# A list scheduler inside the kernel: other costs, a lock between two engines, one engine at a time on a PSUM bank, another margin

## The chip, the cores and the metric

The kernel runs on one core of a Trainium2 chip. The core has five engines that each work through an instruction queue of their own, in order: TensorE (matmuls; PE in the profile, with its weight loads as PEld), VectorE (DVE), ScalarE (ACT), GpSimd (POOL) and SyncE (SP), which here only issues DMAs. An instruction that needs the result of another engine waits for a semaphore, and everything behind it in the same queue waits with it. TensorE writes its results into PSUM, an accumulator memory of eight banks per partition; a bank holds 128 x 512 float32 here. The metric is the time of one execution on the device in microseconds (us), lower is better.

## The reference

One layer of a decoder block on x of 512 tokens by 1024 features, float32. What is computed, cut to the parts that matter here:

```python
xn = rms_norm(x, norm_g)
z = xn @ w_in                                # one wide input projection, split among all below
y_a = fox_attention(rms_norm(qa), rms_norm(ka), va, fa + b_forget)   # 8 heads of 64, causal
y_b = rg_lru(xb, ...)                        # convolution, gates, linear recurrence
y_c = nsa_attention(rms_norm(qc), ...)       # 8 heads: compressed + selected + window attention
y_d = spatial_gating(ud, vd, ...)
ys = [y_a * silu(ga), y_b * silu(gb), y_c * silu(gc), y_d * silu(gd)]
merged = sum(sigmoid(mg[n]) * (ys[n] @ w_branch[n]) for n in range(4))
out = x + merged @ w_out
```

With 512 tokens, the selected attention of y_c takes all blocks and its window covers all keys, so each head of y_c is two ordinary causal attentions (named s and w in the kernel) and one over 31 compressed keys.

## The kernel before, in words

Every float32 operand of a matmul is split into a high part (a copy in the format fp32r) and a low part (operand minus high part), and a product is three matmuls: high by high, low by high, high by low. The split is the steady work of the other engines: ACT or POOL makes the high part, DVE the low part by a subtraction. A weight piece is 128 x 1024, fetched by one DMA of 512 KB into one of four buffers (`raw`), split into one of three pairs (`w`).

**The two kinds of TensorE work.** Dense work is the projections: blocks of 128 x 512 matmuls into a PSUM bank of the pool `z` (three banks), from `zgen` and `chunks`. Attention work is made of units, one per head of y_a (eight, named a) and two per head of y_c (sixteen, s and w). A unit runs: `scores` (matmuls into a bank `s`; DVE adds the mask and takes the maximum; ACT takes the exponential; POOL scales by the reciprocal of the sum, tile `p`), then `finish`: `transposes` in five pieces of two 128 x 128 blocks, each piece into one half of a bank `tb`; for each piece ACT copies the half to `ph` and DVE subtracts to `pl`; then `values` multiplies `ph` and `pl` with v into a bank `o`. `finish` of one unit is interleaved with `scores` of the next, and `fill(gap)` puts a stated amount of dense work between the steps. In the attention of y_a there is one bank `tb` with two halves, in that of y_c there are two banks.

**Who sets the order.** From the first projection to the end of the attention of y_c, the instructions are not issued as the program makes them. `order.on` is true, and every engine call goes to `Order.add`, which records the operation, its cost and what it needs: the operations that wrote or read overlapping areas. At some points (`shut`, and once at the end) `Order.settle` calls `Order.plan` and then issues the operations in the planned order. `plan` is a list scheduler. It keeps for each engine the time from which it is free, takes the engine that can start first, and gives it, among the operations whose needs are met at that time, the one that stands first in the program. An operation is ready when all it needs has ended plus `WAKE` of its own engine (a dictionary of waiting times; 1.2 us for PE, some hundredths for the others, 0.2 for POOL). The costs come from `Order.cost`, linear in the elements of the largest operand. Two matmuls that accumulate into one area have only their order kept, with no wait between them. So the plan's times are never used on the chip, only the order within each queue; the semaphores make it safe. On lines: every planned instruction carries the line of the issuing call in `settle`, L188, in the profile. Work outside the planned region (the warm-up, a few constants, and everything after the attention of y_c: recurrence, spatial gating, merges, output projection) is issued directly and has the line L201 of `_Engine.__getattr__`.

**What a wait covers.** The framework beneath the kernel puts a semaphore wait wherever two engines touch the same data, or the same bank of a PSUM tile, in the order in which the instructions are issued. The planner before knows areas, but neither the bank nor anything that two engines share.

Of the kernel before, what the change touches and what calls it, by code (L numbers as in the profile page):

```python
# [15 lines left out]
PSUM = bass.MemoryType.PSUM  # L16
# [50 lines left out]
class Order:  # L67


    WAKE = {"ACT": 0.036, "DVE": 0.033, "SP": 0.064, "POOL": 0.2, "PE": 1.2}  # L70

    def __init__(self, nc):
        self.eng = {"ACT": nc.scalar, "DVE": nc.vector, "POOL": nc.gpsimd, "PE": nc.tensor, "SP": nc.sync}
        self.on, self.ops, self.seen, self.ring, self.before, self.stacks = False, [], {}, {}, {}, {}
        self.free = dict.fromkeys(self.eng, 0.0)
        self.wire, self.end, self.pending, self.queued = 0.0, {}, [], None

    def pool(self, real, stack):
        p = _Pool(self, real)
        self.stacks.setdefault(id(stack), []).append(p)  # L80
        return p

# [13 lines left out]
    def add(self, name, method, args, kw):  # L96
        aps = [(n == 0, a) for n, a in enumerate(args)] + [(k in ("out", "accum_out"), a) for k, a in kw.items()]
        aps = [(w, a) for w, a in aps if isinstance(a, bass.AP)]
        n, need = len(self.ops), {}
        boxes = [(w, *self.area(a)) for w, a in aps]  # L100
        for w, t, *box in boxes:
            if w and t in self.before:
                need.update((m, True) for m, *_ in self.seen.get(self.before[t], ()))
            for m, w2, b in self.seen.get(t, ()):
                if (w or w2) and box[0] < b[1] and b[0] < box[1] and box[2] < b[3] and b[2] < box[3]:
                    need[m] = need.get(m, False) or not (name == "PE" == self.ops[m][0] and w and w2)
        if self.queued is not None and self.ops[self.queued][0] == name:
# [3 lines left out]
        self.ops.append((name, method, args, kw, need, self.cost(name, kw, aps), {b[1] for b in boxes}))  # L111
        self.pending.append(n)
        return n

    @staticmethod
    def cost(name, kw, aps):

        free = max(a.free_size() for _, a in aps)
        scalar = any(not w and x.free_size() == 1 for w, x in aps)
        if name == "PE":  # L120
            return max(0.112, free / 2400 + 0.018), free / 2400 + 0.175
        if name == "SP":
            return 0.37, aps[0][1].partition_size() * free * 4 / 330e3
        if name == "DVE":
            t, over = 0.17 + free / 850 + 0.06 * scalar, 0.08
        elif name == "ACT":
            t, over = 0.15 + free / 1140 + 0.09 * scalar + 0.12 * ("accum_out" in kw), 0.09
        else:
            two = sum(not w and x.free_size() == free for w, x in aps) > 1
            t, over = (0.3 + free / 430 if two else 0.2 + free / 1100 + 0.1 * scalar), 0.02  # L130
        return t - over, t

    def plan(self):

        ops, left, then, ready = self.ops, {}, {}, {}
        soon, able = {e: [] for e in self.eng}, {e: [] for e in self.eng}
        free, wire, end, out = dict(self.free), self.wire, self.end, []
        for i in self.pending:
            name, need = ops[i][0], ops[i][4]
            ready[i], left[i] = 0.0, 0  # L140
            for m, whole in need.items():
                if m in end:
                    ready[i] = max(ready[i], end[m] + self.WAKE[name] if whole else 0.0)
# [5 lines left out]
        done = {}  # L149
        for _ in self.pending:  # L150
            best = None
            for e in self.eng:
                t = free[e]
                while soon[e] and soon[e][0][0] <= t:
                    heapq.heappush(able[e], heapq.heappop(soon[e])[1])
                c = (t, e) if able[e] else (soon[e][0][0], e) if soon[e] else None
                best = min(best, c) if best and c else best or c
            t, e = best
            while soon[e] and soon[e][0][0] <= t:
                heapq.heappush(able[e], heapq.heappop(soon[e])[1])  # L160
            i = heapq.heappop(able[e])
            busy, whole = ops[i][5]
            free[e] = t + busy
            if e == "SP":
                wire = max(wire, t + 1.6) + whole
                done[i] = wire + 0.6
            else:
                done[i] = t + whole
            out.append((i, t, free[e], wire, done[i]))
            for j in then.get(i, ()):  # L170
                f = ops[j][0]
                ready[j] = max(ready[j], done[i] + self.WAKE[f] if ops[j][4][i] else t)
                left[j] -= 1
                if not left[j]:
                    heapq.heappush(soon[f], (ready[j], j))
        return out

    def settle(self, stack=None):

        if not self.pending:  # L180
            return
        out = self.plan()
        if stack is not None:
            names = {t for p in self.stacks.get(id(stack), ()) for t in p.names}
            out = out[:max((k + 1 for k, o in enumerate(out) if self.ops[o[0]][6] & names), default=0)]
        for i, t, free, wire, done in out:
            name, method, args, kw, *_ = self.ops[i]
            getattr(self.eng[name], method)(*args, **kw)  # L188
            self.free[name], self.wire, self.end[i] = free, wire, done
        gone = {o[0] for o in out}  # L190
        self.pending = [i for i in self.pending if i not in gone]

# [10 lines left out]


class _Pool:
    def __init__(self, order, real):
        self.order, self.real, self.names, self.lines = order, real, [], {}

    def tile(self, *args, tag=None, bufs=None, **kw):
        if tag is not None:  # L210
            kw.update(tag=tag, bufs=bufs)
        t = self.real.tile(*args, **kw)
        self.names.append(t.tensor.name)
        if tag is not None:
# [8 lines left out]
def tile_hybrid_layer(ctx: ExitStack, tc: tile.TileContext, x, xT, units, small, bsp, out):  # L223
    nc = tc.nc
    order = Order(nc)
    ACT, DVE, POOL, PE, DMA = (_Engine(order, e) for e in ("ACT", "DVE", "POOL", "PE", "SP"))

    def pool(name, stack=ctx, **kw):
        return order.pool(stack.enter_context(tc.tile_pool(name=name, bufs=1, reuse_waits="tile", **kw)), stack)


    def behind(op):
# [709 lines left out]
    ug, ready = {}, []  # L942
# [799 lines left out]
```

## Time and profile before

| what | value |
|---|---|
| median of three runs | 725.02 us (724.39 to 725.21) |
| the profiled execution | 724.89 us |
| its span, first to last instruction | 723.2 us |
| TensorE busy | 703.2 us, 97% |
| VectorE busy | 575.8 us, 80% |
| ScalarE busy | 367.2 us, 51% |
| GpSimd busy | 167.7 us, 23% |
| planned region | about 5 to 395 us of the span |

How to read it: the span runs from the first instruction to the last; the execution's own time is 1.7 us longer. A busy share is the union of an engine's instructions as the profiler records them. Matmuls overlap in the records, so that a busy TensorE still can lose some tenths of a microsecond at a wait. A row of the wait view names the waiting engine and tile, the releaser, the total in us, how often, and the longest. A row of the view by windows gives, for one stretch, its length, each engine's busy time with its count of instructions, the granted TensorE clock as a share of full speed, the share of the DMA engines and their GB/s.

### The profile page before, as it was taken

How to read it: one execution, taken by the hardware profiler on the slowest of the kernel's cores; microseconds unless marked ns; L12 is line 12 of the kernel's file. 1: busy time of each engine (PE TensorE's matmuls, PEld its weight loads, DVE VectorE, ACT ScalarE, POOL GpSimd, SP SyncE). 2: the span in 40 equal slices, each digit the busy share in tenths (PEclk: the TensorE clock that was granted, in tenths of full speed). 3: DMA queues.
4: the chain of work that ended last, by engine and by line, in shares of the span. 5: the costliest groups of instructions: out<-in, count | busy, mean ns of one | idle time of the engine just before them, and what ended most of it. 6: DMA issues, size and time to landing. Idle time of an engine off the chain costs nothing.

```text
span 723.2 us, 9672 instructions
## 1 busy us (share of the span) xinstructions
PE 703.2 (97%) x3357; PEld 574.4 (79%) x3357; DVE 575.8 (80%) x1138; ACT 367.2 (51%) x725; POOL 167.7 (23%) x230
## 2 busy tenths in 40 slices
PE   8999999999998999989999999999999999999997
PEld 6888788777866888878887787888888888888876
DVE  6797866666489838888997979999868858958995
ACT  4452565664523336766665891434443551554641
POOL 4115552442445312323343322100000000000000
PEclk9999999999999999999999999999999999999999
DMA  8613222112112521200011223235432242143302
GB/s 321 239 43 116 76 89 70 59 59 76 42 59 88 175 90 57 88 30 30 30 59 43 76 87 102 88 109 182 145 118 88 85 138 98 36 139 117 116 30 87
DMA packets 20640, 68.35 MB, mean 95 GB/s; under 512 B 2416, under 2 KB 2800, under 8 KB 20592
## 3 DMA queue, kind: packets, MB, share of 16 engines
q1 hardware_dynamic: 20160, 67.25, 27.9%
q8 instruction: 26, 0.43, 0.2%
q10 hardware_dynamic: 432, 0.49, 0.2%
q14 instruction: 22, 0.18, 0.1%
HBM read 65.64 MB, written 2.10 MB: 94 GB/s over the span
## 4 chain that ended last, share of the span: by engine, by line
PE 75%; DVE 14%; ACT 8%; issue 2%; DMA 1%; POOL 0%; DVEq 0%; SPq 0%; ACTq 0%
PE pj L201 10%; PE tb L188 4%; PE z_ud L188 3%; PE z_qc L188 3%; PE z_ka L188 3%; PE z_gb L201 3%; PE z_qa L188 3%; PE z_va L188 3%; PE z_mg L201 3%; PE z_xb L188 3%; PE mg2y L201 2%; PE z_kv L188 2%; PE z_vd L188 2%; PE mg3y L201 2%; PE mg1y L201 2%; PE z_gd L188 2%
## 5 line engine op out<-in xcount | busy, mean ns | idle before, releaser
L201 PE MATMUL pj<-w_wb,yh 128*128 128x512 f32 x256 | 80.2, 390 | 0.0
L201 PEld LDWEIGHTS pj<-w_wb,yh 128*128 128x128 f32 x256 | 48.1, 188 | 10.4 <-ACT tm L201 0.4
L201 PE MATMUL pj<-w_wb,yl 128*128 128x512 f32 x128 | 49.8, 389 | 0.0
L188 DVE TENSOR_TENSOR pl_a<-tb,ph_a 128x256 fp32r<-128x256 f32 x40 | 16.1, 421 | 18.7 <-PE tb L188 8.0
L201 DVE TENSOR_TENSOR w_wb<-r_wb,w_wb 128x512 fp32r<-128x512 f32 x32 | 21.8, 713 | 9.5 <-ACT w_wb L201 8.5
L201 PEld LDWEIGHTS pj<-w_wb,yl 128*128 128x128 f32 x128 | 24.0, 188 | 4.9
L188 ACT CAST ph_a<-tb 128x256 fp32r<-128x256 f32 x40 | 14.2, 375 | 25.6 <-PE tb L188 21.9
L188 ACT ACTIVATE p_s<-p_s,nm_s 128x512 f32<-128x512 f32 (+3 forms) x32 | 17.9, 562 | 12.9 <-DVE nm_s L188 12.7
L188 PE MATMUL z_gd<-xh,w_gd 128*128 128x512 f32 x64 | 23.6, 415 | 0.5 <-DVE sgd L188 0.5
L188 POOL TENSOR_SCALAR p_w<-p_w,nm_w 128x128 f32<-128x128 f32 (+3 forms) x32 | 16.9, 546 | 27.1 <-DVE nm_w L188 27.1
L188 POOL TENSOR_SCALAR p_s<-p_s,nm_s 128x128 f32<-128x128 f32 (+3 forms) x32 | 17.2, 556 | 25.3 <-ACT ph_w L188 10.8
L188 DVE CUSTOM_DVE_ANT_0 p_a<-s_a,maskm 128x512 f32<-128x512 f32 (+3 forms) x32 | 15.5, 488 | 9.3 <-PE s_a L188 8.1
L188 PE MATMUL z_xb<-xh,w_xb 128*128 128x512 f32 x64 | 22.9, 415 | 0.0
L188 PE MATMUL z_ud<-xh,w_ud 128*128 128x512 f32 x64 | 22.7, 402 | 0.0
L188 ACT ACTIVATE p_a<-p_a,nm_a 128x512 f32<-128x512 f32 (+3 forms) x32 | 17.9, 561 | 9.4 <-DVE nm_a L188 9.1
L188 PE MATMUL z_ga<-xh,w_ga 128*128 128x512 f32 x64 | 22.0, 404 | 0.0
L188 POOL TENSOR_SCALAR p_a<-p_a,nm_a 128x128 f32<-128x128 f32 (+3 forms) x32 | 18.6, 598 | 14.8 <-DVE nm_a L188 14.8
L188 ACT ACTIVATE p_w<-p_w,nm_w 128x512 f32<-128x512 f32 (+3 forms) x32 | 18.0, 564 | 7.3 <-DVE nm_w L188 6.2
L201 PE MATMUL z_gb<-xh,w_gb 128*128 128x512 f32 x64 | 21.1, 391 | 0.0
L201 ACT CAST w_wb<-r_wb 128x1024 fp32r<-128x1024 f32 x12 | 12.6, 1048 | 15.5 <-issue 15.5
L188 DVE TENSOR_TENSOR pl_s<-tb,ph_s 128x256 fp32r<-128x256 f32 x40 | 16.0, 415 | 4.9 <-ACT ph_s L188 4.6
L188 ACT CAST ph_w<-tb 128x256 fp32r<-128x256 f32 x40 | 13.9, 369 | 11.3 <-PE tb L188 8.9
(812 smaller groups left out, 2336.1 us busy)
## 6 DMA issues: line engine op xcount, KB each, us to landing
r_wb<-in_units_dram SPq DMA_DIRECT2D x16, 512.0 KB, 3.8
xt<-in_x_dram SPq DMA_DIRECT2D x4, 512.0 KB, 8.8
r_ga<-in_units_dram SPq DMA_DIRECT2D x4, 512.0 KB, 3.6
r_gd<-in_units_dram SPq DMA_DIRECT2D x4, 512.0 KB, 3.8
r_ud<-in_units_dram SPq DMA_DIRECT2D x4, 512.0 KB, 4.4
r_gc<-in_units_dram SPq DMA_DIRECT2D x4, 512.0 KB, 3.7
r_xb<-in_units_dram SPq DMA_DIRECT2D x4, 512.0 KB, 3.6
r_gb<-in_units_dram SPq DMA_DIRECT2D x4, 512.0 KB, 3.6
```

Source lines behind the costliest of these rows:

```text
L188: getattr(self.eng[name], method)(*args, **kw)
L201: return lambda *args, **kw: real(*args, **kw).ins
```

## The change

All of it is in the planner; no operation is added to or removed from the kernel, and no engine is changed for any.

- `WAKE` of PE goes from 1.2 to 0.05 us, of POOL from 0.2 to 0.11. A new `MARGIN` adds 0.5 us for PE where the operation waited for is of another compute engine. So a PE operation that waits for DVE, ACT or POOL is ready 0.55 us after its planned end, where it was 1.2.
- `cost` gets other numbers. A PE operation is its columns over 2400 plus the load of its weights; DVE, ACT and POOL get other slopes and constants, POOL two forms. For DVE and POOL it also says whether the operation excludes the other engine: all of POOL but memsets; on DVE those with an operand of more than one element in SBUF and none in PSUM, but not reductions, reciprocals and memsets.
- `plan` keeps `shared`, the end and the engine of the last such operation. One that is placed on the other engine while it runs gets its end put off to after it.
- `plan` keeps `bank`, for each PSUM tile the engine that touched it last and when that ends. An operation of another engine on that tile is put back until then.
- `plan` models TensorE's weight loads by `load`, the time from which the array is free, and the DMA with 350 instead of 330 bytes per ns and other fixed times.

The core of the diff:

```diff
-    WAKE = {"ACT": 0.036, "DVE": 0.033, "SP": 0.064, "POOL": 0.2, "PE": 1.2}
+    WAKE = {"ACT": 0.036, "DVE": 0.033, "SP": 0.064, "POOL": 0.11, "PE": 0.05}
+    MARGIN = {"ACT": 0.0, "DVE": 0.0, "SP": 0.0, "POOL": 0.0, "PE": 0.5}
...
-    @staticmethod
-    def cost(name, kw, aps):
+    def cost(self, name, method, kw, aps):
 
         free = max(a.free_size() for _, a in aps)
         scalar = any(not w and x.free_size() == 1 for w, x in aps)
+        wide = [x for w, x in aps if not w and x.free_size() > 1]
         if name == "PE":
-            return max(0.112, free / 2400 + 0.018), free / 2400 + 0.175
+            weights = kw["lhsT"] if "lhsT" in kw else wide[0]
+            return aps[0][1].free_size() / 2400, 0.112 * max(64, min(128, weights.free_size())) / 128
         if name == "SP":
-            return 0.37, aps[0][1].partition_size() * free * 4 / 330e3
+            return 0.37, aps[0][1].partition_size() * aps[0][1].free_size() * 4 / 350e3
         if name == "DVE":
-            t, over = 0.17 + free / 850 + 0.06 * scalar, 0.08
-        elif name == "ACT":
-            t, over = 0.15 + free / 1140 + 0.09 * scalar + 0.12 * ("accum_out" in kw), 0.09
-        else:
-            two = sum(not w and x.free_size() == free for w, x in aps) > 1
-            t, over = (0.3 + free / 430 if two else 0.2 + free / 1100 + 0.1 * scalar), 0.02
-        return t - over, t
+            alone = bool(wide) and method not in ("tensor_reduce", "reciprocal", "memset") and not any(
+                x.tensor.name in self.psum for x in wide)
+            return 0.155 + free / 960 + 0.05 * scalar + 0.06 * (method == "tensor_tensor_scan" and free / 100), alone
+        if name == "ACT":
+            return 0.15 + free / 1140 + 0.09 * scalar + 0.15 * ("accum_out" in kw), False
+        if method == "memset":
+            return 0.1 + free / 1200, False
+        return (0.09 + free / 540 if len(wide) > 1 and method == "tensor_tensor" else 0.18 + free / 1170), True
+
+    OVER = {"ACT": 0.098, "DVE": 0.082, "POOL": 0.028}
...
+        margin = lambda e, m: self.WAKE[e] + (self.MARGIN[e] if ops[m][0] not in (e, "SP") else 0.0)
...
-            busy, whole = ops[i][5]
-            free[e] = t + busy
-            if e == "SP":
-                wire = max(wire, t + 1.6) + whole
-                done[i] = wire + 0.6
+            open_ = max((bank[x][1] + self.WAKE[e] for x in ops[i][7] if x in bank and bank[x][0] != e), default=0.0)
+            if open_ > t:
+                heapq.heappush(soon[e], (open_, i))
+                continue
+            a, b = ops[i][5]
+            if e == "PE":
+                start = max(t + b, load)
+                load, free[e], done[i] = start + a + 0.014, start + max(a - 0.098, 0.003), start + a + 0.172
+            elif e == "SP":
+                wire = max(wire, t + 1.3) + b
+                free[e], done[i] = t + a, wire + 0.86
             else:
-                done[i] = t + whole
-            out.append((i, t, free[e], wire, done[i]))
+                done[i] = t + a
+                if b:
+                    if shared[1] != e and shared[0] > t + 0.06:
+                        done[i] = shared[0] - 0.06 + a
+                    shared = done[i], e
+                free[e] = done[i] - self.OVER[e]
+            for x in ops[i][7]:
+                bank[x] = e, done[i]
...
-                ready[j] = max(ready[j], done[i] + self.WAKE[f] if ops[j][4][i] else t)
+                ready[j] = max(ready[j], done[i] + margin(f, i) if ops[j][4][i] else t)
```

More of the change, by code (lines that the diff above doesn't have):

```diff
@@ L75, in __init__, with pool @@
         self.free = dict.fromkeys(self.eng, 0.0)
-        self.wire, self.end, self.pending, self.queued = 0.0, {}, [], None
-    def pool(self, real, stack):
-        p = _Pool(self, real)
+        self.wire, self.shared, self.load, self.psum, self.bank = 0.0, (0.0, None), 0.0, set(), {}
+        self.end, self.pending, self.queued = {}, [], None
+    def pool(self, real, stack, psum):
+        p = _Pool(self, real, psum)
         self.stacks.setdefault(id(stack), []).append(p)
@@ L136, in plan @@
         soon, able = {e: [] for e in self.eng}, {e: [] for e in self.eng}
-        free, wire, end, out = dict(self.free), self.wire, self.end, []
+        free, end, out = dict(self.free), self.end, []
+        wire, shared, load, bank = self.wire, self.shared, self.load, dict(self.bank)
+        margin = lambda e, m: self.WAKE[e] + (self.MARGIN[e] if ops[m][0] not in (e, "SP") else 0.0)
         for i in self.pending:
@@ L142, in plan @@
                 if m in end:
-                    ready[i] = max(ready[i], end[m] + self.WAKE[name] if whole else 0.0)
+                    ready[i] = max(ready[i], end[m] + margin(name, m) if whole else 0.0)
                 else:
@@ L148, in plan @@
                 heapq.heappush(soon[name], (ready[i], i))
-        done = {}
-        for _ in self.pending:
+        done, todo = {}, len(self.pending)
+        while len(out) < todo:
             best = None
@@ L161, in plan @@
             i = heapq.heappop(able[e])
-            busy, whole = ops[i][5]
-            free[e] = t + busy
-            if e == "SP":
-                wire = max(wire, t + 1.6) + whole
-                done[i] = wire + 0.6
-            else:
-                done[i] = t + whole
-            out.append((i, t, free[e], wire, done[i]))
+            open_ = max((bank[x][1] + self.WAKE[e] for x in ops[i][7] if x in bank and bank[x][0] != e), default=0.0)
[9 more added lines that the diff above has]
+                free[e], done[i] = t + a, wire + 0.86
+            else:
+                done[i] = t + a
[6 more added lines that the diff above has]
+                bank[x] = e, done[i]
+            out.append((i, dict(free), wire, shared, load, done[i]))
             for j in then.get(i, ()):
                 f = ops[j][0]
-                ready[j] = max(ready[j], done[i] + self.WAKE[f] if ops[j][4][i] else t)
+                ready[j] = max(ready[j], done[i] + margin(f, i) if ops[j][4][i] else t)
                 left[j] -= 1
@@ L185, in settle @@
             out = out[:max((k + 1 for k, o in enumerate(out) if self.ops[o[0]][6] & names), default=0)]
-        for i, t, free, wire, done in out:
+        for i, self.free, self.wire, self.shared, self.load, self.end[i] in out:
             name, method, args, kw, *_ = self.ops[i]
+            self.bank.update((x, (name, self.end[i])) for x in self.ops[i][7])
             getattr(self.eng[name], method)(*args, **kw)
-            self.free[name], self.wire, self.end[i] = free, wire, done
         gone = {o[0] for o in out}
@@ L205, with __init__ @@
 class _Pool:
-    def __init__(self, order, real):
-        self.order, self.real, self.names, self.lines = order, real, [], {}
+    def __init__(self, order, real, psum):
+        self.order, self.real, self.psum, self.names, self.lines = order, real, psum, [], {}
     def tile(self, *args, tag=None, bufs=None, **kw):
@@ L213, in tile @@
         self.names.append(t.tensor.name)
+        if self.psum:
+            self.order.psum.add(t.tensor.name)
         if tag is not None:
@@ L228, in pool @@
     def pool(name, stack=ctx, **kw):
-        return order.pool(stack.enter_context(tc.tile_pool(name=name, bufs=1, reuse_waits="tile", **kw)), stack)
+        return order.pool(stack.enter_context(tc.tile_pool(name=name, bufs=1, reuse_waits="tile", **kw)), stack,
+                          kw.get("space") is PSUM)
     def behind(op):
```

3 lines of the change are left out of this document (2 added, 1 removed).

## The prediction

> **What bounds the kernel now.** I read the page first, then the busy times by windows cut at the kernel's stages, then TensorE's waits by stage, then the order of time around the longest of them. Head of the page, and its chain of waits by engine:
>
> ```profile
> span 723.2 us, 9672 instructions
> PE 703.2 (97%) x3357; PEld 574.4 (79%) x3357; DVE 575.8 (80%) x1138; ACT 367.2 (51%) x725; POOL 167.7 (23%) x230
> PE 75%; DVE 14%; ACT 8%; issue 2%; DMA 1%; POOL 0%; DVEq 0%; SPq 0%; ACTq 0%
> ```
>
> TensorE is busy for 97% of the span and makes up 75% of the chain. A new order cannot take work from it, so the change can win only what TensorE loses now. The windows (stretch, its length, busy PE, PEld, DVE, ACT, POOL, granted clock, DMA) say where that is:
>
> ```profile
> 6.40:85.00 78.60, 77.75 (x341) 62.51 (x342) 63.77 (x110) 36.43 (x61) 29.30 (x31) 1.00 0.42 152
> 85.00:205.00 120.00, 117.19 (x590) 94.95 (x589) 77.27 (x186) 69.09 (x165) 45.80 (x70) 1.00 0.22 71
> 205.00:245.00 40.00, 35.23 (x160) 27.74 (x160) 38.26 (x73) 13.16 (x24) 21.90 (x25) 0.96 0.35 110
> 245.00:270.00 25.00, 25.00 (x121) 20.64 (x121) 12.86 (x36) 7.04 (x18) 3.16 (x3) 1.00 0.36 119
> 270.00:395.00 125.00, 120.64 (x687) 100.06 (x687) 106.90 (x331) 81.44 (x238) 42.55 (x70) 1.00 0.15 47
> ```
>
> These five are the planned region, in order: first projections, attention of y_a, passage to y_c, dense, attention of y_c. TensorE idles 0.85, 2.81, 4.77, 0 and 4.36 us, together 12.8. What follows 395 us is not planned and keeps its order. VectorE has 38.26 of 40 us filled in the passage and 106.90 of 125 in the attention of y_c; in the attention of y_a 77.27 of 120.
>
> TensorE's waits in the region (waiting tile, releaser: total, times, longest), the first seven from the two attentions, the rest from before them and between:
>
> ```profile
> PE tb L188 <- DVE pl_a L188: 1.9, 4, 0.5
> PE tb L188 <- ACT ph_a L188: 0.5, 1, 0.5
> PE s_a L188 <- DVE q_a L188: 0.2, 1, 0.2
> PE tb L188 <- ACT ph_s L188: 1.1, 3, 0.4
> PE tb L188 <- DVE pl_s L188: 1.0, 1, 1.0
> PE tb L188 <- ACT pc L188: 0.8, 1, 0.8
> PE tb L188 <- ACT ph_w L188: 0.4, 2, 0.2
> PE s_s L188 <- DVE q_c L188: 2.9, 1, 2.9
> PE kt_s L188 <- POOL zkm L188: 1.1, 1, 1.1
> PE qt_c L188 <- POOL zq_c L188: 0.3, 1, 0.3
> PE z_kv L188 <- DVE v_a L188: 0.5, 1, 0.5
> PE z_kv L188 <- DVE w_kv.00_743 L188: 0.3, 1, 0.3
> ```
>
> Two families: transposes that wait until another engine has left the bank `tb`, 12 waits and 5.7 us; and work that DVE or POOL delivers late, 6 waits and 5.3 us. A wait costs a little more than its row, since a matmul's record reaches beyond its turn. Rows from the chain (start, length) and from the order of time:
>
> ```profile
> 132.50 2.77 PE z_qc L188 x12
> 133.89 0.76 DVE L188 TENSOR_TENSOR pl_a<-tb,ph_a 128x256 fp32r<-128x256 f32 x2
> 136.02 0.39 PE L188 MATMUL o_a<-pl_a,v_a 128*128 128x512 f32 x1
> ```
>
> Twelve matmuls take 2.77 us, 0.23 each, but one is shown with 0.39: 0.16 of every wait is hidden. (The other two rows are for the margin, below.)
>
> **The change part by part.** No instruction is added or removed, DMAs included, so every term is a wait that goes, comes or moves, and queues other than TensorE's matter only through what they hand to it.
>
> *One engine at a time on a bank.* This is what the first family looks like in order of time:
>
> ```profile
> 116.44 0.37 ACT L188 CAST ph_a<-tb 128x256 fp32r<-128x256 f32 x1 [1.72 <-PE tb L188]
> 116.86 0.33 PE L188 MATMUL tb<-identf,p_a 128*128 128x128 f32 x1
> 117.23 0.42 DVE L188 TENSOR_TENSOR pl_a<-tb,ph_a 128x256 fp32r<-128x256 f32 x1 [1.72 <-PE tb L188]
> 117.71 0.33 PE L188 MATMUL tb<-identf,p_a 128*128 128x128 f32 x1 [0.52 <-DVE pl_a L188]
> ```
>
> ACT reads one half, TensorE writes the first block of the other half, DVE reads the first half, TensorE writes the second block: four turns on one bank where the old plan sees two independent halves. The waits follow the issue order, so TensorE stands at 117.71 with dense matmuls queued behind it. The new plan puts the second block back until the bank is free and gives TensorE a dense matmul meanwhile; nothing is removed from the chain of the unit, since the bank's readers were ahead of it anyway. The family is worth 5.7 + 12 x 0.16 = 7.6 us, with short waits below the view's threshold (the attentions idle 2.81 + 4.36 = 7.2, their rows sum to 5.9 with s_a, some 1.3 more) 8.9. What covers the gain is dense work whose weights are already split; DVE, which splits them, has 43 us to spare in the first attention, but only 18 in the second. I take 70% of 7.6, **-5.3**, between 0 and -8.9.
>
> *The exclusion of DVE and POOL.* The order of time in the passage:
>
> ```profile
> 221.46 1.04 POOL L188 TENSOR_TENSOR zq_c<-zq_c,tsc 128x512 f32<-128x512 f32 x1
> 222.47 1.05 POOL L188 TENSOR_SCALAR w_gd<-r_gd 128x1024 fp32r<-128x1024 f32 x1
> 221.55 0.98 DVE L188 TENSOR_SCALAR sl<-sl 128x4 f32<-128x4 f32 x1
> 222.56 0.96 DVE L188 TENSOR_TENSOR sl<-sl 128x4 f32<-128x4 f32 x1
> 223.56 0.17 DVE L188 TENSOR_SCALAR sl<-sl 128x4 f32<-128x4 f32 x1
> 229.60 0.47 PE L188 MATMUL s_s<-ka_s,q_c 128*128 128x512 f32 x1 [2.86 <-DVE q_c L188]
> 230.60:234.00 3.40, 3.40 (x11) 2.82 (x10) 3.37 (x8) 1.41 (x4) 1.04 (x1) 0.50 0.34 104
> ```
>
> Four elements take DVE 0.98 and 0.96 us while POOL works, 0.17 right after. The old plan books the 0.17, so its DVE runs ahead of the real one, and it sends `s_s` to TensorE's queue 2.86 us too early, in front of dense z_gd. After that standstill the clock is granted at 0.50, the lower of its two levels, for 3.4 us: 1.7 us of work lost.
> The Trainium skill ("SBUF — State Buffer", section "Who interferes with whom") has the same lock: the one that starts first keeps the shared port for its whole instruction, the other stands still. These rows agree, 0.98 against 0.17; what the rule says beyond them comes with the rivals.
> The second family is worth 5.3 + 6 x 0.16 = 6.3 us. Knowing the lock does not shorten it: DVE is full there, and the plan can only fill TensorE's time with other blocks, of which each needs a DVE split too. I take 40%, **-2.5**, between 0 and -6.3; of the clock's 1.7 half, **-0.9**, between 0 and -1.7 (a stall of half the length may still be followed by a slow stretch).
>
> *The margin.* In the rows above, the low part ends at 133.89 + 0.76 = 134.65 and its matmul starts at 136.02, 1.37 later, with dense matmuls between: that is the old 1.2 at work. It goes to 0.55. As long as dense work fills the time, nothing is won by starting 0.65 earlier; at the first scores and first transposes of the two attentions, four places, 4 x 0.65 = -2.6 would be the most. What it may cost: each piece must now be on time within 0.55. The counts of transposes and evictions:
>
> ```profile
> L188 PE MATMUL tb<-identf,p_a x80: 270/272/332, 101.7 to 202.7; 128*128 128x128 f32 x80
> L188 DVE TENSOR_TENSOR pl_a<-tb,ph_a x40: 410/424/426, 104.1 to 203.4; 128x256 fp32r<-128x256 f32 x40
> ```
>
> 80 transposes are 40 pieces for the eight units of y_a; the sixteen units of y_c make 80 more: 120. Today 12 transposes are late, by 0.47 on average. Better costs should make errors smaller, the shorter margin lets more of them through. I take 12 new waits of 0.2 us, **+2.4**; at the upper end 21 of 0.66 (reckoned under the rivals), +13.9.
>
> *Costs of DMA and weight loads.* The first 78.6 us idle for only 0.85 and the diff's total for a 512 KB transfer hardly moves (1.6 + 1.59 + 0.6 against 1.3 + 1.50 + 0.86, all from the diff): **0**, at most +2 if the earlier stages, too, lose cover by the margin: three more waits of the size of z_kv's 0.5 + 0.16.
>
> Sum: -5.3 - 2.5 - 0.9 + 2.4 = -6.3. The profiled execution took 724.89 us (723.2 of span and 1.7 around it), 0.13 below the median of 725.02. So 718.6 on its scale, **718.7** on the median's.
>
> **The rivals.**
> *A, the whole pot.* All late work is foreseen and filled: -8.9 - 6.3 - 1.7 + 2.4 = -14.5, 710.5. For it: most waits stand directly in front of ready dense matmuls, as at 117.71. Against it: DVE's 38.26 of 40 in the passage.
> *B, VectorE sets the pace.* TensorE runs through its dense work sooner and meets unsplit weights later: only the waits of the first attention stay gone, their 1.9 + 0.5 and 5 x 0.16 (-3.2), and the +2.4 of the margin is paid: 724.2. For it: 106.90 of 125. Against it: 18 us of idle VectorE there, and dense z blocks lasting until the end of the region.
> *C, the lock's winner is guessed wrong* (the other side). The place is the handing over of `ph` and `pl` in both attentions. The old 1.2 us covers a whole POOL instruction (1.05); 0.55 does not. If DVE loses the port where the plan has it win, the piece is 1.05 - 0.55 = 0.5 late, and TensorE stands for 0.5 + 0.16. POOL is busy 45.80 of 120 and 42.55 of 125 us, about 36%, so 43 of the 120 pieces are exposed; if half of them lose, 21 x 0.66 = +13.9, and with the gains of -8.7 the time is 730.2. It decides from 8.7 / 0.66 = 13 such pieces on. For it: a matmul that waits takes the whole queue with it. Against it: the plan now knows of the lock at all, and `pl` itself reads PSUM.
> The page named above states what C rests on: who blocks is decided by which of the two is issued first, not by the kind of operation. The rows cannot show how often two queues come in the planned order.
>
> **How the numbers follow.** Forecast 0.47 (its own range 715 to 722), A 0.18, B 0.17, C 0.18. A measurement of this kernel can tell about 0.2%, 1.45 us, from no change. Faster: the forecast but for 0.02, all of A, a fifth of B: 0.66. Same: the rest of B and the forecast's 0.02, less 0.02 of B: 0.14. Slower: C and that 0.02: 0.20. The range goes from A's 710.5 to 729, short of C's end, and leaves out about 0.07 below and 0.10 above.
>
> **What would show it.** Right: of the `tb` rows about four waits and under 2 us are left; the wait of `s_s` for `q_c` is under 1.5 us; idle TensorE from 6.4 to the end of the region falls from 12.8 to 8; low parts are used some 0.6 after they end, not 1.4. B: the `tb` waits are gone, and in their place dense `z` matmuls wait for DVE. C: more `o` and `tb` waits than now, short, with DVE as releaser. Wrong in kind: `tb` still waits 12 times for half a microsecond, which would mean that the bank was not the cause; or the time is gained or lost after the planned region.

## The result, and the profile after

The changed kernel takes 716.2 us (median of 4 runs, 715.04 to 716.98) beside 724.9 us for the kernel before; the ratio is 0.9879, with a 95% interval of 0.9862 to 0.9897. By the ratio that is 8.8 us, 1.2%, faster. The forecast of 718.7 us was 2.5 us too high, and the sign and the range held. The experiments will show that the closeness of the sum is in part luck: one of its terms was wrong by 5 us, and the terms do not add.

The profiled execution took 716.89 us with a span of 715.2. The head of its page:

```profile
span 715.2 us, 9666 instructions
PE 700.1 (98%) x3357; PEld 573.8 (80%) x3357; DVE 571.3 (80%) x1138; ACT 365.3 (51%) x725; POOL 174.1 (24%) x230
```

The same 3357 matmuls are in it. The span is 8.0 us shorter: TensorE's idle time went from 723.2 - 703.2 = 20.0 to 715.2 - 700.1 = 15.1 us, and its "busy" time lost 3.1 us. No matmul became faster; the record of a matmul that is followed by a wait or has just waited is longer than its turn (the 0.16 us of the prediction), so fewer stalls also show as less busy time.

The windows (stretch, its length, then busy PE, PEld, DVE, ACT, POOL, granted clock, DMA share, GB/s):

```profile
6.40:85.00 78.60, 77.02 (x337) 61.65 (x338) 63.21 (x109) 36.31 (x61) 31.28 (x31) 1.00 0.41 151
85.00:205.00 120.00, 118.20 (x603) 97.66 (x601) 79.76 (x193) 69.69 (x167) 50.27 (x74) 1.00 0.22 71
205.00:245.00 40.00, 36.52 (x164) 28.60 (x165) 35.23 (x73) 12.72 (x26) 22.49 (x22) 0.96 0.41 132
245.00:270.00 25.00, 25.00 (x128) 20.76 (x127) 12.66 (x37) 6.85 (x19) 2.11 (x3) 1.00 0.33 105
270.00:387.00 117.00, 116.19 (x669) 96.94 (x668) 103.33 (x324) 79.44 (x234) 43.27 (x70) 1.00 0.15 46
```

TensorE now idles 1.58, 1.80, 3.48, 0 and 0.81 us, together 7.7, where it was 12.8. Most of that came from the last stage, the attention of y_c: 4.36 to 0.81.

Since the windows cut at fixed times, the stages are better compared by landmarks. These are rows of single tiles, first before, then after; behind the count stand the shortest, median and longest duration in ns, and then the starts of the first and the last of them. The four landmarks are the end of the first projections, of the attention of y_a, of dense z_gd, and of the attention of y_c:

```profile
L188 PE MATMUL z_va<-w_va.11_204,uh x16: 389/392/497, 71.7 to 77.1; 128*128 128x512 f32 x16
L188 DVE TENSOR_TENSOR y_a<-o_a,ol_a x8: 672/682/684, 113.2 to 207.3; 64x512 f32<-64x512 f32 x8
L188 PE MATMUL z_gd<-xh,w_gd x64: 387/395/629, 219.7 to 252.5; 128*128 128x512 f32 x64
L188 DVE TENSOR_TENSOR y_c<-o_s,ol_c x8: 670/683/685, 291.1 to 396.7; 64x512 f32<-64x512 f32 x8
```

```profile
L211 PE MATMUL z_va<-w_va.11_204,uh x16: 389/391/497, 72.7 to 78.1; 128*128 128x512 f32 x16
L211 DVE TENSOR_TENSOR y_a<-o_a,ol_a x8: 676/683/684, 112.3 to 202.1; 64x512 f32<-64x512 f32 x8
L211 PE MATMUL z_gd<-xh,w_gd x64: 387/395/628, 205.2 to 249.7; 128*128 128x512 f32 x64
L211 DVE TENSOR_TENSOR y_c<-o_s,ol_c x8: 674/683/684, 287.6 to 388.7; 64x512 f32<-64x512 f32 x8
```

Dense matmuls may be done in one stage or in the next, so the length of a stage alone tells little. For each stage I take its length from landmark to landmark and subtract its work: every matmul in it by its columns, 0.227 us for 512, 0.067 for 128 and in proportion between, the distances at which they follow one another in the trace when nothing stands between. What remains is lost time, in us (e1, e2 and e11 are experiments below):

| stage | before | change | e1 | e2 | e11 |
|---|---|---|---|---|---|
| first projections | 5.5 | 6.5 | 6.1 | 6.4 | 6.2 |
| attention of y_a | 15.2 | 11.5 | 21.1 | 13.7 | 8.6 |
| passage, with z_gd | 9.3 | 9.0 | 6.3 | 11.3 | 7.8 |
| dense and attention of y_c | 23.6 | 18.5 | 27.0 | 21.4 | 17.7 |
| merge and all behind | 9.4 | 9.4 | 9.0 | 9.0 | 8.8 |

Each of these five profiles has one stretch of 3.4 us at a granted clock of 0.50 before its merge, which costs about 1.7 us (half of it) wherever it falls: in the passage before the change, in the change and in e11, but in the attention of y_a in e1 (from 85.0 us) and e2 (from 83.7).

The attention of y_a lost 130.2 - 115.0 = 15.2 us before and loses 124.0 - 112.5 = 11.5 now; that of y_c 144.2 - 120.6 = 23.6 and 139.0 - 120.5 = 18.5. These two make up -3.7 and -5.1, and with +1.0 at the start and -0.3 in the passage the sum is -8.1, the difference of the spans (-8.0). So the gain lies in the two attentions, where the bank rule acts. In the passage, whose long wait was to go by the exclusion, nothing to speak of was won.

TensorE's waits in the planned region, in the same view as before the change (the rest are 0.3 to 0.8 us each, dense blocks that wait for `v_a`, `sgd` or a split weight):

```profile
PE tb L211 <- DVE pl_a L211: 1.3, 2, 0.9
PE kt_s L211 <- POOL zkm L211: 1.2, 1, 1.2
...
PE z_gd L211 <- ACT w_gd L211: 0.8, 1, 0.8
...
PE tb L211 <- POOL p_s L211: 0.6, 2, 0.3
...
PE tb L211 <- DVE pl_s L211: 0.3, 1, 0.3
PE tb L211 <- DVE pl_w L211: 0.2, 1, 0.2
```

The rows of `tb` fell from 12 waits and 5.7 us to 6 and 2.4. The wait of `s_s` for `q_c` (2.9) is gone. In its place stand short waits of dense blocks for their split weights, such as the 0.8 us of z_gd and another 0.8 of z_ka.

The same piece of the same attention as in the prediction, in order of time (start, length, engine, what):

```profile
115.02 0.65 ACT L211 CAST ph_a<-tb 128x256 fp32r<-128x256 f32 x2 [0.35 <-PE tb L211]
115.70 0.76 DVE L211 TENSOR_TENSOR pl_a<-tb,ph_a 128x256 fp32r<-128x256 f32 x2 [0.82 <-ACT ph_a L211]
116.67 0.39 PE L211 MATMUL z_qc<-w_qc.00_775,xl 128*128 128x512 f32 x1
116.90 0.38 PE L211 MATMUL tb<-identf,p_a 128*128 128x128 f32 x2
117.03 0.48 PE L211 MATMUL o_a<-pl_a,v_a 128*128 128x512 f32 x1
117.34 0.38 PE L211 MATMUL tb<-identf,p_a 128*128 128x128 f32 x2
```

Both of ACT's reads and both of VectorE's stand behind one another now, and TensorE comes back to the bank at 116.90, after VectorE has left it at 115.70 + 0.76 = 116.46. Meanwhile it works on z_qc and waits for nothing. The low part is used at 117.03, 0.57 after its end, where it was 1.37: the shorter margin at work.

### The profile page after: what moved, and what is told of

Same layout as the page of the kernel before. It is cut to its first block, busy times and chain, and to the rows that moved or that the text cites. A ratio compares the mean times of both kernels' runs of the same rounds, so it can differ in the third digit from the quotient of the medians.

```text
span 715.2 us, 9666 instructions
## 1 busy us (share of the span) xinstructions
PE 700.1 (98%) x3357; PEld 573.8 (80%) x3357; DVE 571.3 (80%) x1138; ACT 365.3 (51%) x725; POOL 174.1 (24%) x230
## 4 chain that ended last, share of the span: by engine, by line
PE 74%; DVE 16%; ACT 6%; issue 2%; POOL 1%; DMA 1%; SPq 0%; DVEq 0%; ACTq 0%; POOLq 0%
PE pj L223 8%; PE z_ud L211 3%; PE z_qc L211 3%; PE z_qa L211 3%; PE tb L211 3%; PE z_va L211 3%; PE z_gd L211 3%; PE z_mg L223 3%; PE z_ga L211 2%; PE mg2y L223 2%; PE z_vd L211 2%; PE mg3y L223 2%; PE mg1y L223 2%; PE z_ka L211 2%; PE z_kv L211 2%
## 5 line engine op out<-in xcount | busy, mean ns | idle before, releaser
L223 PEld LDWEIGHTS pj<-w_wb,yh 128*128 128x128 f32 x256 | 48.1, 188 | 10.4 <-ACT tm L223 0.5
L211 PE MATMUL z_gd<-xh,w_gd 128*128 128x512 f32 x64 | 23.6, 421 | 1.6 <-ACT w_gd L211 0.8
L211 ACT ACTIVATE p_s<-p_s,nm_s 128x512 f32<-128x512 f32 (+3 forms) x32 | 17.9, 560 | 11.3 <-DVE nm_s L211 10.9
L211 POOL TENSOR_SCALAR p_a<-p_a,nm_a 128x128 f32<-128x128 f32 (+3 forms) x32 | 19.9, 638 | 11.4 <-DVE nm_a L211 10.7
L223 PE MATMUL z_gb<-xh,w_gb 128*128 128x512 f32 x64 | 21.1, 390 | 0.0
L211 DVE TENSOR_TENSOR pl_w<-tb,ph_w 128x256 fp32r<-128x256 f32 x40 | 15.6, 418 | 3.4 <-ACT ph_w L211 3.0
```

The costliest lines, as they stand in the source:

```text
L223: return lambda *args, **kw: real(*args, **kw).ins
```

## The experiments

The change has four parts: the rule for a bank, the exclusion ("lock"), the new costs of all engines, and the margin. The kernels below put them together in different ways. The last column is (ratio - 1) x 725 us, so that runs on different chips compare; the 95% intervals of the ratios reach 0.001 to 0.002 to either side, 0.7 to 1.6 us.

| run | bank rule | lock | costs | margin us | median us | ratio | us against before |
|---|---|---|---|---|---|---|---|
| the change | yes | yes | new | 0.55 | 716.21 | 0.9879 | -8.8 |
| e1_no_bank | no | yes | new | 0.55 | 731.05 | 1.0072 | +5.2 |
| e2_no_lock | yes | no | new | 0.55 | 724.04 | 0.9979 | -1.5 |
| e3_margin_115 | yes | yes | new | 1.20 | 718.94 | 0.9911 | -6.5 |
| e4_only_bank | yes | no | old | 1.20 | 720.29 | 0.9926 | -5.4 |
| e5_only_margin | no | no | old | 0.55 | 727.32 | 1.0030 | +2.2 |
| e6_only_costs | no | no | new | 1.20 | 730.08 | 1.0067 | +4.9 |
| e7_costs_lock | no | yes | new | 1.20 | 727.66 | 1.0035 | +2.5 |
| e9_margin_045 | yes | yes | new | 0.50 | 718.00 | 0.9907 | -6.7 |
| e10_margin_075 | yes | yes | new | 0.80 | 713.73 | 0.9850 | -10.9 |
| e11_old_dve_cost | yes | yes | new, VectorE's old | 0.55 | 709.98 | 0.9795 | -14.9 |
| e12_bank_short_margin | yes | no | old | 0.55 | 721.52 | 0.9954 | -3.3 |

(The margin is MARGIN and WAKE of TensorE together. e8 is the kernel before once more.)

**e1, the change without the bank rule.**

```diff
-            open_ = max((bank[x][1] + self.WAKE[e] for x in ops[i][7] if x in bank and bank[x][0] != e), default=0.0)
-            if open_ > t:
-                heapq.heappush(soon[e], (open_, i))
-                continue
```

> The changed kernel (716.2 us) without the rule of one engine at a time on a PSUM bank; costs, lock and margin stay. If the bank rule makes the gain (the two attentions together came out 9 us shorter with the change, the other stages not): 722 to 725 us, with about twelve waits of tb back. If better costs and the lock of VectorE and GpSimd make it: at most 718. If the gain is the chance of a reshuffled order: anything from 713 to 722, without a pattern in the tb waits.

Measured 731.05 us, ratio 1.0072 (1.0057 to 1.0087): slower than before by 5.2 us, and 14 us slower than the change, beyond every value that had been expected. Its waits, and the landmarks of the two attentions:

```profile
PE tb L207 <- DVE pl_a L207: 2.5, 7, 0.6
...
PE tb L207 <- DVE pc L207: 1.7, 2, 1.6
...
PE z_kv L207 <- DVE w_kv.00_743 L207: 2.4, 1, 2.4
```

```profile
L207 DVE TENSOR_TENSOR y_a<-o_a,ol_a x8: 676/684/686, 115.8 to 211.2; 64x512 f32<-64x512 f32 x8
...
L207 DVE TENSOR_TENSOR y_c<-o_s,ol_c x8: 673/680/685, 294.4 to 403.2; 64x512 f32<-64x512 f32 x8
```

All its `tb` rows together are 26 waits and 10.4 us, against 6 and 2.4 in the change and 12 and 5.7 before. The attention of y_a ends 9.1 us later than in the change, that of y_c 14.5 later, and by the table of lost time the two attentions lose 9.6 and 8.5 us more (the passage 2.7 less). Not all of this is the bank. At the start of the attention of y_a, `z_kv` waits 2.4 us for VectorE's low part of a weight (0.3 in the change), and the stretch at the lower clock stands here instead of in the passage: about 4 of the 9.6 us. The rest is as the bank's family would have it: taking the rule away brings the waits for the bank back, in the stages where they stood. There are more of them than before the change, where the rule was missing too: the old costs and the old margin had kept part of them from showing.

**e2, the change without the lock.**

```diff
-                if b:
+                if False:
```

> The changed kernel without the exclusion of VectorE and GpSimd in the plan; its costs, the bank rule and the margin stay. If the bank rule makes the gain: 716 to 718, since the passage between the attentions, where the lock shows most, gained nothing. If the lock makes it: 721 to 725, with late q_c and late pl in the attentions. If the shorter margin only works because the lock is known: 719 to 722, with many short waits of o and tb.

Measured 724.04 us, ratio 0.9979 (0.9969 to 0.9990), 7.3 us worse than the change, in the range expected if the lock makes the gain. Its waits, its window of the passage, and its VectorE there in order of time:

```profile
PE kt_s L211 <- POOL zkm L211: 3.5, 2, 2.6
PE hpsk L211 <- DVE w_w1k L211: 2.8, 1, 2.8
PE s_s L211 <- DVE q_c L211: 2.1, 1, 2.1
```

```profile
205.00:245.00 40.00, 31.35 (x148) 24.05 (x147) 35.80 (x69) 11.40 (x21) 21.26 (x23) 1.00 0.33 105
```

```profile
217.18 1.00 DVE L211 TENSOR_TENSOR sl<-sl 128x4 f32<-128x4 f32 x1
...
218.79 0.96 DVE L211 TENSOR_TENSOR sl<-sl 128x4 f32<-128x4 f32 x1
```

The operations on four elements again stand in the middle of POOL's run and take up to a microsecond. In the change the plan does all but one of them from 232.9 us on, most of them in a pause of POOL, at 0.14 to 0.18 us each for the first four. TensorE idles 8.65 us in this window, against 3.48 in the change. By the table of lost time the lock is worth 2.2, 2.3 and 2.9 us in the attention of y_a, the passage and the attention of y_c. With the 1.7 us of the lower clock taken out of both kernels these become 0.5, 4.0 and 2.9: the lock acts in the passage, where its long waits show, and in the attention of y_c. Part of the 7.3 us is the clock as well: the median of the mean granted clocks is 0.995 in e2's runs and 0.998 in the change's, and by the kernel before (0.997 against 1.000, 1.5 us) I estimate 1.5 us for that. The `tb` rows are as few as in the change (6 waits, 1.9 us), so the first family of waits does not need the lock to stay away, as the prediction had it.

**e3, the change with the old margin.**

```diff
-    MARGIN = {"ACT": 0.0, "DVE": 0.0, "SP": 0.0, "POOL": 0.0, "PE": 0.5}
+    MARGIN = {"ACT": 0.0, "DVE": 0.0, "SP": 0.0, "POOL": 0.0, "PE": 1.15}
```

> The changed kernel with the margin of TensorE at 1.15, so that it waits for 1.2 us as before; all else stays. By the prediction's term for the margin (+2.4 for new short waits): 713.5 to 714.5, with the late w_ka.01 of 0.7 us at 13.9 us gone. If the shorter margin is a part of the gain, since TensorE's chain is shorter: 718 to 722. If it hardly matters: 716.

Measured 718.94 us, ratio 0.9911 (0.9895 to 0.9928), 2.3 us worse than the change. But its planned region is not longer. Its last wait, and VectorE at the end of the region, first e3, then the change:

```profile
PE g L223 <- DVE xcl L223: 2.1, 2, 1.8
```

```profile
387.45 0.68 DVE L211 TENSOR_TENSOR y_c<-o_s,ol_c 64x512 f32<-64x512 f32 x1 [1.29 <-ACT ol_c L211]
388.20 2.54 DVE L223 TENSOR_TENSOR w_mg00.10_4167<-r_mg00.10_4165,w_mg00.10_4167 128x512 fp32r<-128x512 f32 x2
```

```profile
387.50 0.68 DVE L223 TENSOR_TENSOR w_mg00.10_4167<-r_mg00.10_4165,w_mg00.10_4167 128x512 fp32r<-128x512 f32 x1
388.67 0.68 DVE L211 TENSOR_TENSOR y_c<-o_s,ol_c 64x512 f32<-64x512 f32 x1 [0.50 <-ACT ol_c L211]
```

The last y_c is 1.2 us earlier in e3 than in the change. Behind it VectorE splits a weight of the merge (2.54 us for two instructions, which otherwise take 0.68 each), and the `xcl` that the matmuls of `g` need next stands behind that. In the change the split was done among the last pieces of the attention. Reckoned as in the table, the lost time of e3 from the start to the last y_c is the change's within 0.2 us, and behind it 2.0 us more. What the shorter margin "gained" here is a hand-over behind the planned region that happens to fall well.

**e4, the bank rule alone.** The kernel before, with the rule (the lines that e1 takes out) and nothing else; TensorE comes back 0.05 us after a bank is free.

> The kernel before (724.9 us) with the bank rule alone; old costs, no lock, old 1.2 us. If the bank rule makes the gain: 716 to 719, with the tb waits gone and the wait of s_s for q_c (2.9 us) still there. If it needs the costs beside it: 721 to 724. If it does nothing: 724 to 726.

Measured 720.29 us, ratio 0.9926 (0.9911 to 0.9940): -5.4 us, between the value expected if the rule makes the gain by itself and the one if it needs the costs. Five `tb` waits with 2.4 us are left. The long wait of the passage is still there (2.9 us before), though shorter:

```profile
PE s_s L197 <- DVE q_c L197: 1.8, 1, 1.8
```

**e5, the short margin alone, on the kernel before.**

```diff
-    WAKE = {"ACT": 0.036, "DVE": 0.033, "SP": 0.064, "POOL": 0.2, "PE": 1.2}
+    WAKE = {"ACT": 0.036, "DVE": 0.033, "SP": 0.064, "POOL": 0.2, "PE": 0.55}
```

> The kernel before (724.9 us) with 0.55 in place of 1.2 us for TensorE, and nothing else. If the old 1.2 us was cover for what the old plan does not know (lock and bank), as the 731.1 us without the bank rule suggests: 729 to 734, with more than 20 waits of tb and o. If a shorter wait is a gain by itself: 721 to 723. If it hardly matters: 724 to 726.

Measured 727.32 us, ratio 1.0030 (1.0016 to 1.0043): +2.2 us. The `tb` rows are 17 waits and 5.6 us, so there are more and shorter ones than before's 12 and 5.7; the largest of its rows is

```profile
PE tb L188 <- DVE pl_a L188: 3.4, 9, 0.6
```

where before had 1.9 us in 4 waits. The loss is less than what had been expected from a lost cover. Reckoned as in the table, the attention of y_a, where the waits for `pl_a` stand, loses 3.6 us more than before, and the passage 3.0 less, of which 1.7 is the stretch at the lower clock: this execution, the fastest of ten (725.05 us), has none.

**e6, the new costs alone**, with the old margin and neither rule (the edits of e1, e2 and e3 together; it also keeps what has no run of its own: POOL's `WAKE` of 0.11, the model of TensorE's weight loads, and 0.05 in place of 1.2 us where TensorE waits for a DMA), and **e7, the new costs with the lock** (the edits of e1 and e3).

> The new costs of the operations (and of weight loads and DMA) alone: no bank rule, no lock, TensorE waits for 1.2 us. If the costs by themselves are worth something: 720 to 723. If they are only the ground for the other parts: 724 to 726. If DVE booked shorter than before makes the plan too early where POOL is in the way: 727 to 731.

> New costs and the lock, TensorE waits for 1.2 us, no bank rule. Against the run with the new costs alone it shows the lock without the short margin. If the lock is worth its 8 us only where the margin is short: within 2 us of the costs alone. If it is worth them anywhere: 6 to 9 us less than the costs alone. The wait of s_s for q_c (2.9 us before) should be gone in either case.

e6 measured 730.08 us, ratio 1.0067 (1.0045 to 1.0089), +4.9 us; e7 727.66, ratio 1.0035 (1.0022 to 1.0048), +2.5. The new costs by themselves make the kernel slower, and the lock gives back 2.4 us of it, though the two intervals touch. That is close to the 2 us expected if the lock is worth more only beside a short margin; the wait of `s_s` for `q_c`, expected to go, fell from 2.2 to 0.8 us. Waits of e6:

```profile
PE kt_s L207 <- POOL zkm L207: 2.9, 3, 2.2
...
PE s_s L207 <- DVE q_c L207: 2.2, 1, 2.2
```

They are waits for VectorE and POOL, and that of `kt_s` has grown from 1.1 to 2.9 us. The `tb` rows grew from 12 waits and 5.7 us to 19 and 8.6.

**e8, the kernel before once more**, to see what the same program does twice.

> The kernel before, unchanged, profiled once more. In the profile before, the first projections ended at 77.48 us (last matmul of z_va), in the five changed kernels profiled so far at 78.06 to 78.83. If that is the changed order: 77.3 to 77.7 again. If it is the arrival of the first DMAs, whose order is the same in all: anywhere from 77.4 to 79.

It took 725.45 us with a span of 723.7, 0.5 more than the profiled execution of before, and all of these 0.5 us lie ahead of the end of the first projections; every landmark behind is shifted by the same 0.5. So of the +1.0 with which the changed kernel begins, half may be the scatter that one program shows.

**e9 and e10, the change with two other margins**: 0.45 and 0.75 in place of 0.5 in the line that e3 changes.

> The changed kernel with the margin of TensorE at 0.45 instead of 0.5. Nothing but the order of the planned work can differ. If the size of the margin acts as a cause (theory: shorter hands the work over earlier, up to the point where pieces come late), a step of 0.05 is worth 2.7 x 0.05 / 0.65 = 0.2 us, and the time is 715.5 to 717, with the same waits. If a plan of this kind is partly a throw of dice (rival: every small shift makes another order, and which late hand-overs it meets is chance), the time lies anywhere from 713 to 720, with other waits than those of the changed kernel.

> The changed kernel with the margin of TensorE at 0.75, between the 0.5 of the change (716.2) and the 1.15 of the earlier run (718.9). If the gain of the shorter margin is a steady function of its size, 717.2 (716.7 to 718). If the 2.7 us between those two came from one place, the hand-over from the planned region to the merge, it is all or nothing: about 716 with the splits of w_mg among the last unit of the second attention, or about 719 with g waiting for xcl after the region. Dice: anywhere from 713 to 721.

e9 measured 718.00 us, ratio 0.9907 (0.9891 to 0.9922); e10 713.73, ratio 0.9850 (0.9834 to 0.9865). In the order of margins, 0.50, 0.55, 0.80 and 1.20 us, the times are 718.0, 716.2, 713.7 and 718.9: not a steady function, and each of e9 and e10 lies where only chance had been expected to put it. e9 differs from the change by 0.05 us in one constant and by 2.1 us by the ratios, though the intervals of these two overlap. It lost at the same place as e3:

```profile
PE g L223 <- DVE xcl L223: 1.1, 1, 1.1
```

e10 does the split of that weight early, as the change does, and has in the passage neither the waits of z_gd for its weights above 0.3 us nor a stretch at the lower clock. Its four runs have mean clocks of 0.999 to 1.0, so part of its 2.1 us over the change is this stretch. The four margins fit the reading that each plan is partly a throw of dice: a small shift gives another order, and whether it meets such a late hand-over or such a stretch is worth some 2 us to either side.

**e11, the change with VectorE's old cost.**

```diff
-            return 0.155 + free / 960 + 0.05 * scalar + 0.06 * (method == "tensor_tensor_scan" and free / 100), alone
+            return 0.17 + free / 850 + 0.06 * scalar + 0.06 * (method == "tensor_tensor_scan" and free / 100), alone
```

> The changed kernel with VectorE's costs as the old plan booked them (0.17 + n/850 + 0.06 with a scalar; 0.77 for 512 elements against 0.69 in the new costs), all else as changed. The new costs by themselves lost 4.9 us in an earlier run. If that loss comes from VectorE being booked shorter, so that the plan runs ahead of the real VectorE, the old cost gains here: 711 to 715, with fewer waits for VectorE and POOL. If the exclusion and the bank rule already make the plan true, the longer cost only makes it late: 716.5 to 719. If the loss of the new costs came from TensorE's or the DMAs' costs, no difference, 715.5 to 717.

Measured 709.98 us (708.77 to 711.05), ratio 0.9795 (0.9774 to 0.9816): 14.9 us faster than before and 6.1 faster than the change, more than any expectation had. It is the best kernel of this study. Its page, and the longest of its waits:

```profile
span 709.2 us, 9669 instructions
PE 698.5 (98%) x3357; PEld 575.3 (81%) x3357; DVE 568.9 (80%) x1138; ACT 365.7 (52%) x725; POOL 170.8 (24%) x230
```

```profile
PE s_s L211 <- DVE q_c L211: 1.5, 1, 1.5
```

No wait of `tb` is left in that view. Idle TensorE fell from 15.1 to 709.2 - 698.5 = 10.7 us. By the table of lost time 2.9 of the gain lie in the attention of y_a, 1.2 in the passage and 0.8 in the attention of y_c. The old formula books 512 elements on VectorE with 0.77 us, the new one with 0.69. An undisturbed instruction of that size takes 0.68 in the trace (the rows of e3 above), so the new one is the truer for it; but the splits of w_gd in the change are

```profile
L211 DVE TENSOR_TENSOR w_gd<-r_gd,w_gd 128x512 fp32r<-128x512 f32 x8 | 6.9, 885 | 0.3 <-ACT w_gd L211 0.2
```

with a mean of 0.885 us: the median of these eight is 0.70, and the longest took 1.53.

**e12, the bank rule with the short margin**, on the kernel before, with the old costs and without the lock (the edits of e4 and e5).

> The kernel before with the bank rule (720.3 in an earlier run) and with TensorE's wait at 0.55 instead of 1.2; costs and exclusion as before. If the bank rule is what makes a short margin harmless (theory: without it a short margin lost 2.2 us on the kernel before and 3.4 on the new costs, with it the full change won 2.7), the time is 717 to 720.3. If the exclusion is what a short margin needs (rival: without it pieces meet POOL on the port and come late), it is 722 to 725, and the new rows are waits for pl or z blocks whose VectorE work stood behind POOL.

Measured 721.52 us, ratio 0.9954 (0.9936 to 0.9971). That lies between the two expectations: the short margin costs 2.1 us beside the bank rule (-5.4 to -3.3), as much as without it (+2.2). The `tb` rows are only 5 waits and 1.9 us, so the bank is not why. The loss is in the passage, in one wait and what follows it:

```profile
PE s_s L197 <- DVE q_c L197: 3.5, 1, 3.5
```

That was 1.8 us in e4. More weighs the clock: its mean over 205 to 245 us is 0.87 (0.96 in e4), 10.2 us at 0.50 in place of 3.4, so 3.4 us more lost, which is above the whole difference of 2.1. All four runs have mean clocks of 0.992 to 0.995, those of e4 0.998.

## Why the prediction was right, and where it was not

**The bound.** Right. TensorE's work is unchanged, and the gain is idle TensorE in the planned region: 12.8 to 7.7 us, where 8 was predicted; nothing was gained behind the region (9.4 us lost there in both).

**The bank rule, -5.3.** Right for the part alone: -5.4 (e4). The mechanism is as it was told: dense matmuls fill the time, the chain of the unit does not get longer, six `tb` waits with 2.4 us are left ("about four and under 2" was said). But within the change the same rule is worth 14 us (e1): under the other parts its family had grown from 12 waits to 26, and some 2 of the 14 are the late weight named there.

**The exclusion, -2.5.** Right in size beside the new costs alone (-2.4, e6 to e7), and 7.3 us within the change (e2). (The prediction's list of this family left out one wait in the passage, `z_gd` for `sgd`, 0.5 us, which the change still has; with it 40% would be 2.8.) The means was the predicted one: the plan puts other work in the place of operations that would stand still, the wait of `s_s` is gone. Against before the passage has won only 0.3 us of lost time, though. There the lock makes up for what the new costs lose, and short waits for split weights came in place of the long one.

**The clock, -0.9.** Not shown to be an effect of the change. Of its four runs, two have spans of 715.2 and 715.3 with a mean granted clock of 0.997, and two 713.3 and 713.8 with 1.0 and 0.999; the median stands between them. But the kernel before does the same: of the nineteen executions beside e5 to e8, eight had a mean clock of 1.0 (723.3 to 724.4 us) and eleven 0.995 to 0.998 (725.1 to 727.3). What this gives to a median of four runs is chance.

**The margin, +2.4.** Right in size where it stands alone (+2.2, e5) and beside the bank rule (+2.1, e12), but the mechanism is only half of it. The term stood for twelve new short waits; in e5 those for `pl_a` went from 4 to 9, while all `tb` rows together kept their 5.6 us, and in e12 the clock outweighs the rest. That the size fits twice is in part luck. Within the whole change the sign is the other one (e3 is 2.3 us slower with the longer margin), but by the hand-over to the merge, not by the attentions: the prediction's term held nothing behind the region. By e9 and e10 that figure is not a law of the margin's size.

**The costs, 0 to +2.** This is the step that failed: a term that was put near nothing. The prediction spoke of "costs of DMA and weight loads" only and found that nothing in the first 78.6 us depends on them. The term measured +4.9 us (e6). The new VectorE costs, which the diff also holds, were not priced. By e11 these lose 6.1 us within the change. Whether they make up all of e6's 4.9 was not tried: e6 was not run with VectorE's old cost, nor were the costs of the other engines, POOL's shorter `WAKE` or the model of the weight loads tried apart.

**The sum, -6.3.** Measured alone or in steps, the parts give -5.4 - 2.4 + 2.2 + 4.9 = -0.7; together they give -8.8. The sum came out only 2.5 us off because a term that was missed (+4.9) and an interaction that was not thought of (-8.1) partly cancel; that is luck. With plans that scatter by some 2 us each, the -8.1 is uncertain by several us; that there is an interaction rests on the 14 and the 7.3 us of e1 and e2, against 5.4 and 2.4. I read it as follows. Before, coarse costs and a long margin covered part of the bank's and the port's delays; the change takes both covers away and puts the true rules in their place. Removing a cover without the rule costs (e1, e2), and a rule under the old cover wins less (e4).

**The rivals.** A, the whole pot (710.5): not what the change did, but the pot was there, since e11 reached 710.0. B, VectorE sets the pace: refuted. VectorE fills 103.33 of 117 us in the last stage (88%, 86% before), and the only waits for it there are 0.3 and 0.2 us of `tb`. C, the lock's winner is guessed wrong: refuted. 13 late pieces of 0.66 us were its point of decision, and the view of waits shows four for VectorE's low parts, 1.8 us together.

**Why VectorE's longer cost wins** is argued, not shown. A cost above the undisturbed 0.68 us leaves the plan a reserve on the engine that hands TensorE its work, where single instructions take much longer than that (1.53 us for one of w_gd, 2.54 for two of the merge's split in e3). How much of the 6.1 us is the luck of one order is open: the steps of the margin moved the time by 2.1 to 4.4 us by the ratios.

## What to carry to other kernels

In a planned order, a constant that is too long is often a cover for a rule that the plan lacks: when costs are made exact and margins short, price each cover that goes, not only each rule that comes. Test the parts alone and left out, since here the four parts, measured alone or in steps, give -0.7 us and together -8.8. And when a constant shifts the whole order, a difference of some 2 us (0.3%) between two values says little: look first whether it came from one late hand-over, and try neighbouring values before a value is called better.

## What was not expected of the hardware

The prediction tied the lower clock to the standstill before it (2.86 us, then 0.50). A long standstill is there at the fall in e1 (2.4 us) and e12 (3.5 us), too, but in the change none is, and not every standstill brings a fall. Windows of the passage, first the change, then e2:

```profile
230.00:235.00 5.00, 4.63 (x27) 3.69 (x25) 4.85 (x17) 3.78 (x10) 1.65 (x4) 1.00 0.83 248
235.00:236.00 1.00, 0.57 (x3) 0.20 (x2) 0.97 (x2) 0.95 (x3) 0.91 (x2) 1.00 0.88 311
236.00:237.00 1.00, 0.60 (x3) 0.50 (x4) 1.00 (x3) 0.86 (x2) 0.83 (x3) 1.00 0.70 283
237.00:238.00 1.00, 1.00 (x4) 0.81 (x3) 1.00 (x2) 0.00 (x0) 1.00 (x1) 0.52 0.27 111
```

```profile
225.00:230.00 5.00, 2.90 (x14) 1.93 (x12) 4.89 (x10) 0.29 (x1) 0.00 (x0) 1.00 0.00 0
230.00:235.00 5.00, 5.00 (x29) 4.17 (x28) 4.97 (x19) 4.24 (x11) 1.67 (x2) 1.00 0.39 113
```

In the change no wait ahead of the fall is longer than 0.5 us: TensorE worked 4.63 of 5 us, then 1.17 of 2, and the clock fell. In e2 it stayed at 1.00 through five us of which TensorE worked 2.90. The plainest case is e5: there `s_s` waits 2.9 us for `q_c` as in the kernel before, and the clock stayed at 1.00 behind it. By their mean clocks of 1.0 and 0.999, two of the four runs of the change, the same program, have no such stretch either. What decides it, these runs do not show.
